# A list scheduler that merges threads by estimated times: new prices for returns to dense products, copies that count as readers, and three reorderings inside the threads

## The chip, the core and the metric

The kernel runs on one core of one Trainium2 chip. TensorE (PE) multiplies and transposes; its weight loads are shown on a line of their own (PEld). VectorE (DVE), ScalarE (ACT) and GpSimd (POOL) do the element-wise work, and most transfers between device memory and on-chip memory are issued by SyncE (SP). The metric is the time of one execution on the device in microseconds (us). The time before is the median of three runs.

## What is computed

One step of a two-layer decoder for a prompt of 2048 positions (16 tiles of 128) and 64 sample positions (8 sequences of 8), model width 1024. Both groups share all weights.

```python
# layer 0 (even): gated DeltaNet, 4 heads, beside sliding-window attention, 8 query heads / 2 kv heads
qkv_a, gate_a, a_in, b_in, q_b, k_b, v_b, gate_b = jnp.split(x @ w_in, EVEN_SPLITS, axis=-1)
qkv_a, new_conv = causal_conv(qkv_a, conv_buf, conv_w)
...
o_a, new_s = gated_delta_rule(q_a, k_a, v_a, log_decay, beta, s0)      # chunkwise, a triangular inverse per chunk
o_a = rms_norm(o_a, norm_g).reshape(n, l, A_VW) * jax.nn.silu(gate_a)
...
y = jnp.concatenate([o_a, o_b], axis=-1) @ w_out
# layer 1 (odd): HGRN2, 8 heads, 128 x 128 state each
dec = masked_exp(causal, G_c[:, :, :, None, :] - G_c[:, :, None, :, :])
a = jnp.einsum('nhid,nhijd,nhjd->nhij', q_c, dec, k_c)
o = jnp.einsum('nhid,nhde->nhie', q_c * jnp.exp(G_c), s) + jnp.einsum('nhij,nhje->nhie', a, v_c)
...
# after each layer
h = layer_norm(DEEPNORM_ALPHA * x + y, g, b)
return h + jax.nn.sigmoid(h @ w_ple_gate) * (p @ w_ple_proj)
```

The outputs are both activations and all new states and caches.

## The kernel before

**Threads and their merge.** The work is written as Python generators ("threads"), and each yields one instruction at a time. While the program is built, a loop in `run` (L525) chooses which thread goes next, so the order in which instructions stand in each engine's queue is the order in which this loop emits them. On the chip each engine then follows its own queue in order, and waits on semaphores where it needs another's result. The loop keeps an estimated clock for each engine, and for each buffer the estimated time of its last write and of its last reads. `op` (L348) gives each instruction a cost and a list of buffers read and written, `start` (L422) the earliest estimated start, and `emit` (L446) advances the clocks. Of all pending instructions the one with the lowest score goes next. For TensorE the score is the start with 700 ns of margin added to each input it reads (MARGIN, L57), less a price for a change between array modes.

**Three kinds of TensorE work.** Dense products have 128 x 128 weights and fp32r operands; a product is split in three, since each operand is held as a high and a low part. Full-size products that are not dense are the transposes (against the constant `ident`, in the trace bank<-cst,ar) and the fp32 products of the recurrences. Small products use 32 or 64 rows or columns of the array (`prod`, `sums`, `inverse`). `SWITCH` (L58) prices the change of array mode: 213 to whole, 100 to small. `STAY` (L59) adds 1000 ns to the score of whatever would lead from small back to whole. So a small product is taken ahead of a dense one even if it is ready somewhat later. The dense thread has the lowest priority: its score carries LATER, 30 ns.

**Threads of the even layer.** `dense_delta` makes four dense products for each of the 4 heads and each of 5 groups of tiles (2 or 4 tiles). `conv` consumes three of them and `dgate` one. `delta_unit` then runs `delta_core` (L1274): transposes of k and q, a ScalarE square of each 128 x 128 tile with the row sum as accumulator output (the squares go to one scrap buffer, `junk`), the decays, a triangular inverse in `inverse` (L1356: small products, a ScalarE copy, small products, a copy under a mask, for each of four sizes), the scan over the tiles, and `rms_out` (L1465), which squares again into a scrap buffer, scales, transposes and multiplies by the gate.

**Threads of the odd layer.** `hgrn_unit` runs once for each of 8 heads and 5 groups of tiles, so 40 times, at most three at a time (UNITS, L52). Its core is `hgrn_core` (L1716). `scale(s)` there multiplies one half of q and one half of k in place by running products B of the decays, and then makes the next, half as long B from it; the next scale starts with that B. `level(ps, c0, s)` copies small products under a mask into the diagonal blocks `Dv`. Between the scales of 32 and of 128 stand two ScalarE copies (KC and QC), three levels (4, 8, 16) and the scale of 64.

**After each layer.** `dense_post` makes the output projection, the norm, and the gate of the embedding; it is almost all dense products with transposes in `post_norm`.

**Memory.** An arena of 50 blocks of 1024 columns is handed out while the loop runs. There are eight PSUM banks, three of them (BANKS, L55) for dense products and five for the rest.

Of the kernel before, what the change touches and what calls it, by code (L numbers as in the profile page):

```python
# [54 lines left out]
BANKS = 3  # L55
LATER = 30
MARGIN = 700  # L57
SWITCH = {True: 213, False: 100}  # L58
STAY = 1000  # L59
WHOLE = (128, 128)  # L60
SMALL = (1, 2, 4, 8, 16)

# [74 lines left out]
def bc(ap, axis, n):  # L137

    ap = ap.unsqueeze(axis)
    shape = list(ap.shape)  # L140
    shape[axis] = n
    return ap.to_broadcast(shape)
# [24 lines left out]


class Op:
    __slots__ = ("eng", "fn", "cost", "rd", "wr", "tab", "nbytes", "mode", "place", "port")  # L170


class Ask:
# [35 lines left out]
class Sched:  # L209
    def __init__(self, tc):  # L210
        self.tc, self.nc = tc, tc.nc
        self.engines = {e: getattr(tc.nc, e) for e in ("tensor", "vector", "scalar", "gpsimd", "sync")}
        self.clk = dict.fromkeys(self.engines, 0.0)
        self.dma = 0.0
        self.tab = 0
        self.mode, self.place = WHOLE, None
        self.port = 0.0
        self.keys = {}
        self.threads = []
        self.pools = []  # L220
        self.seq = 0
        self.blocks, self.bi = [], {}
        self.mask, self.avail, self.owner = [], [], {}
        self.free_cols = 0
        self.parts = {}
        self.banks, self.bank_key = {}, {}
        self.dirty = True
        self.cur = None
# [119 lines left out]
    def op(self, eng, m, kw):  # L348
        o = Op()
        o.eng = eng  # L350
        o.tab = 0
        o.nbytes = 0
        f = getattr(self.engines[eng], m)
        o.fn = lambda: f(**kw)  # L354
        rd, wr = [], []
        src = None
        for k, v in kw.items():
            if hasattr(v, "ap") and hasattr(v, "offset"):
                if k in ("out", "accum_out", "ap"):
                    wr.append(self.key(v))  # L360
                    if k != "accum_out":
                        out = v
                else:
                    rd.append(self.key(v))
                    if src is None:
                        src = v
        o.rd, o.wr = rd, wr
        sh = out.shape
        n = 1
        for d in sh[1:]:  # L370
            n *= d
        ps_in = any(hasattr(v, "ap") and hasattr(v, "offset") and v.name in self.bank_key for k, v in kw.items() if k not in ("out", "accum_out"))
        if eng == "tensor":
            lhs = kw["in_"] if m == "transpose" else kw["lhsT"]
            o.mode = tuple(32 if x <= 32 else 64 if x <= 64 else 128 for x in (lhs.shape[0], lhs.shape[1]))
            o.place = (lhs.offset // lhs.ap[0][0], out.offset // out.ap[0][0])
            load = o.mode[1] * 0.84 + 3
            if m == "transpose":
                o.cost = max(load, n * 0.835 + 2)
            elif kw["rhs"].dtype == F32R:  # L380
                o.cost = max(load, n * 0.4258 + 8)
            else:
                o.cost = max(2 * load, n * 1.74)
        elif eng == "scalar":
            o.cost = n * 0.8333 + (51 if ps_in else 93)
            for k in ("bias", "scale"):
                if hasattr(kw.get(k), "ap"):
                    o.cost += 93
            if "accum_out" in kw:
                o.cost += 93  # L390
            o.tab = TABLE.get(kw["func"], 0)
        elif eng == "vector":
            if m in ("tensor_copy", "memset"):
                o.cost = n * (1.04 if ps_in else 0.52) + 68
            elif m == "tensor_scalar":
                o.cost = n * (1.04 if ps_in else 0.52) + 130
            elif m == "scalar_tensor_tensor":
                o.cost = n * 1.04 + 130
            elif m == "reciprocal":
                o.cost = n * 6.25 + 70  # L400
            elif m == "bn_stats":
                o.cost = 602
            else:
                o.cost = n * 1.04 + 69
        elif eng == "gpsimd":
            if m == "tensor_tensor":
                o.cost = (165 * n + 100) if kw["op"] == ALU.pow else 2.1 * n + 148
            elif m == "tensor_scalar":
                o.cost = 0.83 * n + 245
            elif m == "tensor_copy":  # L410
                o.cost = 3.4 * n + 100
            else:
                o.cost = 0.6 * n + 100

        two = sum(hasattr(kw.get(k), "ap") and kw[k].name not in self.bank_key for k in ("in_", "in0", "in1")) - (m == "transpose")
        o.port = eng == "gpsimd" and m in ("tensor_tensor", "tensor_copy") or eng == "vector" and (two == 2 or two == 1 and m in ("tensor_copy", "tensor_scalar") and out.name not in self.bank_key)
        if m == "dma_start":
            o.cost = 475.0 if eng == "sync" else 1320.0
            o.nbytes = 4 * n * sh[0]
        return o  # L420
# [25 lines left out]
    def emit(self, o, t):  # L446
        o.fn()
        c = o.cost
        if o.eng == "tensor":
            if o.mode == self.mode != WHOLE and o.place != self.place:  # L450
                c = 20 if o.mode[0] == 32 else c / 2 if o.place[1] <= self.place[1] else 14
            self.mode, self.place = o.mode, o.place
        if o.tab and not (self.tab & o.tab):
            c += 1283
        if o.tab:
# [69 lines left out]
    def run(self):  # L525
        while self.threads:
# [6 lines left out]
            for t in self.threads:  # L533
                o = t.pend
                if not isinstance(o, Op):
                    continue

                s = self.start(o, MARGIN if o.eng == "tensor" else 0, True)
                if o.eng == "tensor" and self.mode != o.mode:
                    s -= SWITCH[o.mode == WHOLE] - STAY * (o.mode == WHOLE)  # L540
                sc = s + (1283 if o.tab and not (self.tab & o.tab) else 0) + (t.prio >= 1e6) * LATER
                if best is None or sc < best[0]:
                    best = (sc, s, t)
# [9 lines left out]
def al(n, r=False):  # L553

    return Ask("mem", (n, r))
# [22 lines left out]
class Step(Sched):  # L578
# [695 lines left out]
    def delta_core(self, np_, n, cs, q, G4, maskD, small, out, own):  # L1274
# [5 lines left out]
        WT = n * 128  # L1280
        sm = yield al(128)
        ss, Gp, Gj, kds, lqk = sm[:np_, 0 : 2 * n], sm[:np_, 8 : 8 + n], sm[:np_, 16 : 16 + n], sm[:np_, 24 : 24 + n], sm[:np_, 32 : 32 + n]
        junk = yield al(128)
        psk = yield bank()
        for c in range(n):
            yield self.P.transpose(out=psk[:np_, c * 128 : (c + 1) * 128], in_=kT[:, c * cs : (c + 1) * cs], identity=self.ident)
        for c in range(n):
            yield self.A.activation(out=junk[:np_], in_=psk[:np_, c * 128 : (c + 1) * 128], func=AF.Square, accum_out=ss[:, c : c + 1])
        psq = yield bank()
        for c in range(n):  # L1290
            yield self.P.transpose(out=psq[:np_, c * 128 : (c + 1) * 128], in_=qT[:, c * cs : (c + 1) * cs], identity=self.ident)
        for c in range(n):
            yield self.A.activation(out=junk[:np_], in_=psq[:np_, c * 128 : (c + 1) * 128], func=AF.Square, accum_out=ss[:, n + c : n + c + 1])
        self.freebank(psq)
        self.free(junk)
        yield self.A.activation(out=ss, in_=ss, func=AF.Ln, bias=self.eps[:np_])
        lk, lq = ss[:, :n], ss[:, n:]
        yield self.V.scalar_tensor_tensor(out=Gp, in0=lk, scalar=-0.5, in1=G, op0=ALU.mult, op1=ALU.add)
# [15 lines left out]
        yield self.A.activation(out=lqk, in_=lqk, func=AF.Exp)  # L1314
        yield self.V.scalar_tensor_tensor(out=Gj, in0=lk, scalar=0.5, in1=GmB, op0=ALU.mult, op1=ALU.add)

        kdb = yield al(WT)
        kd = cut(kdb[:np_], 128)
        yield self.V.tensor_tensor(out=kd, in0=cut(psk[:np_, :WT], 128), in1=bc(kds, 2, 128), op=ALU.mult)
        self.freebank(psk)  # L1320
# [144 lines left out]
    def rms_out(self, np_, n, cs, po, lqk, g, sg, dst):  # L1465


        sm = yield al(256)
        f, junk = sm[:np_, 128 : 128 + n], sm[:np_, 0:128]
        for c in range(n):  # L1470
            yield self.A.activation(out=junk, in_=po[:np_, c * 128 : (c + 1) * 128], func=AF.Square, accum_out=f[:, c : c + 1])
        if lqk is not None:
            yield self.V.scalar_tensor_tensor(out=f, in0=lqk, scalar=EPS * 128 * 128, in1=f, op0=ALU.mult, op1=ALU.add)
        else:

            yield self.V.tensor_scalar(out=f, in0=f, scalar1=EPS * 128 * 4 * 128, scalar2=None, op0=ALU.add)
        yield self.G.tensor_tensor(out=f, in0=f, in1=self.mhalf[:np_, :n], op=ALU.pow)
        on = yield al(n * 128)
        yield self.V.tensor_tensor(out=cut(on[:np_], 128), in0=cut(po[:np_, : n * 128], 128), in1=bc(f, 2, 128), op=ALU.mult)
        for c in range(n):  # L1480
            yield self.P.transpose(out=po[:, c * cs : (c + 1) * cs], in_=on[:np_, c * 128 : (c + 1) * 128], identity=self.ident[:np_, :np_])
# [234 lines left out]
    def hgrn_core(self, np_, n, cs, q, k, f, deep, out, own):  # L1716
# [14 lines left out]
        def scale(s):  # L1731
# [3 lines left out]
            qv = QF.rearrange("p (b r i) -> p b r i", r=2, i=hs)  # L1735
            kv = k.rearrange("p (b r i) -> p b r i", r=2, i=hs)
            bv = B.rearrange("p (b r) -> p b r", r=2)
            yield self.V.tensor_tensor(out=qv[:, :, 1, :], in0=qv[:, :, 1, :], in1=bc(bv[:, :, 0], 2, hs), op=ALU.mult)
            yield self.V.tensor_tensor(out=kv[:, :, 0, :], in0=kv[:, :, 0, :], in1=bc(bv[:, :, 1], 2, hs), op=ALU.mult)
            if Bs is None:  # L1740
                Bs = yield al(W)
            B = Bs[:, bo : bo + nbk]
            bo += nbk
            yield self.V.tensor_tensor(out=B, in0=bv[:, :, 0], in1=bv[:, :, 1], op=ALU.mult)

        def prod(ps, c0, kk, qq):

# [60 lines left out]
        if deep:  # L1808
# [16 lines left out]
            KC, QC = (cut(KB[:, i * W // 2 : (i + 1) * W // 2], 32) for i in range(2))  # L1825
            yield self.A.activation(out=KC, in_=k.rearrange("p (b r i) -> p b r i", r=2, i=32)[:, :, 0, :], func=AF.Copy)
            yield self.A.activation(out=QC, in_=right(QF, 32), func=AF.Copy)
            for i, s in enumerate((4, 8, 16)):
                yield from level(ps, i * n * 16, s)
            self.freebank(ps)  # L1830
            yield from scale(64)
            ps = yield bank()
            for c in range(n):
                for b in range(2):
# [359 lines left out]
```

## Time and profile before

| | |
|---|---|
| median of three runs | 3127.14 us (3126.95 to 3135.73) |
| profiled execution | 3119.46 us; span from first to last instruction 3117.7 us |
| mean granted TensorE clock | 0.983 |
| instructions | 63598 |
| PE busy / PEld busy | 3002.6 us / 2498.8 us |
| DVE busy / ACT busy / POOL busy | 1964.8 us / 1228.3 us / 198.7 us |

The even layer's mixers take roughly the first 1200 us, its projection the time to about 1600 us, the odd layer's mixers the time to about 2700 us, and its projection the rest. In the profile all instructions stand under one line, L354, since one helper records each of them; they are told apart by engine, operation and shape. "128*32 128x16" of a TensorE row is the part of the array that is used, then the moving operand. A duration of a matmul there is its passage through the pipeline, not its share of the engine: consecutive starts are much closer together.

### The profile page before, as it was taken

The page shows a single profiled execution, that of the slowest core. Times are in us where ns is not written, and L with a number is a line of the kernel's source. Part 1 is how long each engine was busy: PE and PEld are TensorE (multiplying, and loading weights), DVE is VectorE, ACT ScalarE, POOL GpSimd, SP SyncE. Part 2 cuts the span into 40 slices and gives each one's busy share as a digit, 9 for nine tenths or more (in the row PEclk, how much of TensorE's full clock was granted, in tenths as well). Part 3 has the DMA queues.
Part 4 walks back from the last instruction along what each step waited for, and adds up shares of the span by engine and source line. Part 5 has one row for each costly group of instructions (what it writes and reads, how often), then busy time and mean ns, then how long its engine had stood idle before and what let it go on. Part 6 is the DMA issues. An engine that isn't in the chain of part 4 may idle for free. (4 is left out here: it accounts for less than half of the span.)

```text
span 3117.7 us, 63598 instructions
## 1 busy us (share of the span) xinstructions
PE 3002.6 (96%) x25592; PEld 2498.8 (80%) x25592; DVE 1964.8 (63%) x5693; ACT 1228.3 (39%) x3314; POOL 198.7 (6%) x265
## 2 busy tenths in 40 slices
PE   8999999999999999999999999998999999999999
PEld 7887778877787787878888888887888888787787
DVE  5567776786767675333367786868577677733333
ACT  4555555564556462101144343434444444411011
POOL 0000000000000001111100000000000000111110
PEclk9999999999999999999999999999999999999999
DMA  4221132231214154333332121222221122732331
GB/s 119 71 77 47 47 92 63 71 80 44 68 54 114 48 171 138 87 79 88 88 112 64 49 63 49 76 64 87 70 59 56 44 70 61 213 87 75 83 86 49
DMA packets 320838, 246.45 MB, mean 79 GB/s; under 512 B 33800, under 2 KB 285840, under 8 KB 320528
## 3 DMA queue, kind: packets, MB, share of 16 engines
q1 hardware_dynamic: 253408, 207.80, 22.0%
q0 software_dynamic: 67136, 34.61, 6.2%
q8 instruction: 200, 3.28, 0.4%
q14 instruction: 94, 0.77, 0.1%
HBM read 182.98 MB, written 60.45 MB: 78 GB/s over the span
## 5 line engine op out<-in xcount | busy, mean ns | idle before, releaser
L354 PE MATMUL bank<-ar,ar 128*128 128x512 f32 (+10 forms) x20432 | 2813.2, 302 | 67.2 <-ACT ar L354 39.8
L354 PEld LDWEIGHTS bank<-ar,ar 128*128 128x128 f32 (+4 forms) x20432 | 2244.8, 162 | 474.2 <-ACT ar L354 65.1
L354 ACT ACTIVATE ar<-bank 128x128 f32<-128x128 f32 (+13 forms) x1471 | 525.9, 368 | 1081.5 <-PE bank L354 998.6
L354 DVE TENSOR_TENSOR ar<-ar,ar 128x256 f32<-128x256 f32 (+8 forms) x1500 | 732.6, 517 | 247.9 <-ACT ar L354 210.3
L354 ACT ACTIVATE ar<-ar 128x512 f32<-128x512 f32 (+15 forms) x1067 | 527.8, 522 | 750.0 <-DVE ar L354 384.6
L354 DVE SCALAR_TENSOR_TENSOR ar<-ar,bank 128x512 f32<-128x512 f32 (+3 forms) x256 | 164.1, 641 | 386.6 <-ACT ar L354 254.2
L354 PE MATMUL bank<-cst,ar 128*128 128x128 f32 (+3 forms) x1439 | 239.7, 279 | 27.5 <-DVE ar L354 16.4
L354 PEld LDWEIGHTS bank<-cst,ar 128*128 128x128 f32 (+3 forms) x1439 | 173.5, 141 | 73.8 <-DVE ar L354 16.9
L354 POOL TENSOR_TENSOR ar<-ar,mhalf 128x2 f32<-128x2 f32 (+3 forms) x104 | 109.2, 1050 | 1496.8 <-DVE ar L354 1130.1
L354 DVE TENSOR_TENSOR ar<-bank,ar 128x128 fp32r<-128x128 f32 (+7 forms) x326 | 147.2, 455 | 75.7 <-ACT ar L354 43.7
L354 DVE TENSOR_TENSOR ar<-ar 128x4 f32<-128x4 f32 (+10 forms) x592 | 139.9, 250 | 19.9 <-ACT ar L354 13.3
L354 DVE SCALAR_TENSOR_TENSOR ar<-bank,ar,ar 128x509 f32<-128x509 f32 (+8 forms) x216 | 122.7, 573 | 25.8 <-ACT ar L354 24.4
L354 DVE SCALAR_TENSOR_TENSOR ar<-ar,ar,bank 128x128 f32<-128x128 f32 x192 | 65.8, 343 | 115.2 <-PE bank L354 114.6
L354 PEld LDWEIGHTS bank<-ar 32*32 32x32 f32 (+3 forms) x2640 | 88.8, 121 | 38.9 <-ACT ar L354 13.6
L354 PE MATMUL bank<-ar 32*32 32x32 f32 (+5 forms) x2640 | 113.7, 209 | 4.5 <-ACT ar L354 2.3
L354 DVE COPY_PREDICATED ar<-cst,bank 128x64 f32<-128x64 uint32 (+3 forms) x356 | 85.9, 242 | 34.9 <-PE bank L354 24.4
L354 DVE SCALAR_TENSOR_TENSOR ar<-ar,ar,ar 128x1024 f32<-128x1024 f32 (+1 forms) x68 | 87.0, 1280 | 13.8 <-POOL ar L354 13.8
L354 POOL MEMSET ar<- 128x256 f32 (+4 forms) x85 | 29.1, 348 | 961.1 <-PE bank L354 550.6
L354 DVE SCALAR_TENSOR_TENSOR ar<-ar,ar 128x4 f32<-128x4 f32 (+10 forms) x190 | 58.4, 312 | 31.7 <-ACT ar L354 30.5
L354 POOL DMA_DIRECT2D ar<-os x64 | 57.3, 898 | 296.9 <-PE bank L354 197.0
L354 ACT ACTIVATION_READ_ACCUMULATOR ar<-bank 128x1 f32 (+1 forms) x340 | 66.2, 195 | 0.0
L354 ACT ACT_TABLE_LOAD x49 | 62.9, 1283 | 5.5 <-DVE ar L354 4.0
(55 smaller groups left out, 799.9 us busy)
## 6 DMA issues: line engine op xcount, KB each, us to landing
ar<-os POOLq DMA_DIRECT2D x64, 512.0 KB, 5.0
ar<-in_w_in_odd SPq DMA_DIRECT2D x64, 512.0 KB
ar<-in_w_in_even SPq DMA_DIRECT2D x60, 512.0 KB
os<-ar SPq DMA_DIRECT2D x36, 512.0 KB
ar<-x SPq DMA_DIRECT2D x32, 512.0 KB
os<-ar SPq DMA_DIRECT2D x56, 256.0 KB
ar<-in_x_prompt SPq DMA_DIRECT2D x16, 512.0 KB
ar<-in_w_ple_gate SPq DMA_DIRECT2D x16, 512.0 KB
```

What stands on the lines that cost most here:

```text
L354: o.fn = lambda: f(**kw)
```

## The change

It alters the merge's prices and three places in the threads. No instruction is added or taken away.

1. Prices. `SWITCH` becomes 105 to whole and 120 to small. A new mark `dense` on each TensorE instruction tells fp32r products of whole size from all others. A dense product that follows one that was not dense is charged `BACK`, 90 ns, on the estimated clock. `STAY` becomes a pair: 900 ns on the score of what leads from small to whole, and 300 ns on the score of a dense product that follows a whole-size one that is not dense.
2. A copy under a mask (`copy_predicated`) is now listed as a reader of its own output, so that the estimate lets it start 127 ns after the last write of that buffer on the same engine.
3. In `delta_core` and `rms_out` the squares no longer share one 128-column scrap: each goes to a slice of its own in a buffer that is needed later anyway (`kdb`, `on`), which is allocated earlier for it.
4. In `scale` the running product B is made between the multiplication of q and that of k.
5. In `hgrn_core` the three masked levels and the three instructions of the scale of 64 are interleaved, a scale first.

```diff
-SWITCH = {True: 213, False: 100}
-STAY = 1000
+SWITCH = {True: 105, False: 120}
+BACK = 90
+STAY = (900, 300)
...
+        if m == "copy_predicated":
+            rd.append(self.key(kw["out"]))
...
+            o.dense = o.mode == WHOLE and m != "transpose" and kw["rhs"].dtype == F32R
...
-            self.mode, self.place = o.mode, o.place
+            if o.dense and not self.was_dense:
+                c += BACK
+            self.mode, self.place, self.was_dense = o.mode, o.place, o.dense
...
-                if o.eng == "tensor" and self.mode != o.mode:
-                    s -= SWITCH[o.mode == WHOLE] - STAY * (o.mode == WHOLE)
+                if o.eng == "tensor":
+                    if self.mode != o.mode:
+                        s -= SWITCH[o.mode == WHOLE] - STAY[0] * (o.mode == WHOLE)
+                    elif o.dense and not self.was_dense:
+                        s += STAY[1]
...
-        junk = yield al(128)
+        kdb = yield al(WT)
...
-            yield self.A.activation(out=junk[:np_], in_=psk[:np_, c * 128 : (c + 1) * 128], func=AF.Square, accum_out=ss[:, c : c + 1])
+            yield self.A.activation(out=kdb[:np_, c * 128 : (c + 1) * 128], in_=psk[:np_, c * 128 : (c + 1) * 128], func=AF.Square, accum_out=ss[:, c : c + 1])
...
-        sm = yield al(256)
-        f, junk = sm[:np_, 128 : 128 + n], sm[:np_, 0:128]
+        sm = yield al(128)
+        f = sm[:np_, :n]
+        on = yield al(n * 128)
         for c in range(n):
-            yield self.A.activation(out=junk, in_=po[:np_, c * 128 : (c + 1) * 128], func=AF.Square, accum_out=f[:, c : c + 1])
+            yield self.A.activation(out=on[:np_, c * 128 : (c + 1) * 128], in_=po[:np_, c * 128 : (c + 1) * 128], func=AF.Square, accum_out=f[:, c : c + 1])
...
-            yield self.V.tensor_tensor(out=qv[:, :, 1, :], in0=qv[:, :, 1, :], in1=bc(bv[:, :, 0], 2, hs), op=ALU.mult)
-            yield self.V.tensor_tensor(out=kv[:, :, 0, :], in0=kv[:, :, 0, :], in1=bc(bv[:, :, 1], 2, hs), op=ALU.mult)
...
+            yield self.V.tensor_tensor(out=qv[:, :, 1, :], in0=qv[:, :, 1, :], in1=bc(bv[:, :, 0], 2, hs), op=ALU.mult)
             yield self.V.tensor_tensor(out=B, in0=bv[:, :, 0], in1=bv[:, :, 1], op=ALU.mult)
+            yield self.V.tensor_tensor(out=kv[:, :, 0, :], in0=kv[:, :, 0, :], in1=bc(bv[:, :, 1], 2, hs), op=ALU.mult)
...
-            for i, s in enumerate((4, 8, 16)):
-                yield from level(ps, i * n * 16, s)
+            masked = iter([level(ps, i * n * 16, s) for i, s in enumerate((4, 8, 16))])
+            for o in scale(64):
+                yield o
+                yield from next(masked)
             self.freebank(ps)
-            yield from scale(64)
```

More of the change, by code (lines that the diff above doesn't have):

```diff
@@ L169 @@
 class Op:
-    __slots__ = ("eng", "fn", "cost", "rd", "wr", "tab", "nbytes", "mode", "place", "port")
+    __slots__ = ("eng", "fn", "cost", "rd", "wr", "tab", "nbytes", "mode", "place", "port", "dense")
 class Ask:
@@ L215, in __init__ @@
         self.tab = 0
-        self.mode, self.place = WHOLE, None
+        self.mode, self.place, self.was_dense = WHOLE, None, True
         self.port = 0.0
@@ L1292, in delta_core @@
         for c in range(n):
-            yield self.A.activation(out=junk[:np_], in_=psq[:np_, c * 128 : (c + 1) * 128], func=AF.Square, accum_out=ss[:, n + c : n + c + 1])
+            yield self.A.activation(out=kdb[:np_, c * 128 : (c + 1) * 128], in_=psq[:np_, c * 128 : (c + 1) * 128], func=AF.Square, accum_out=ss[:, n + c : n + c + 1])
         self.freebank(psq)
-        self.free(junk)
         yield self.A.activation(out=ss, in_=ss, func=AF.Ln, bias=self.eps[:np_])
@@ L1315, in delta_core @@
         yield self.V.scalar_tensor_tensor(out=Gj, in0=lk, scalar=0.5, in1=GmB, op0=ALU.mult, op1=ALU.add)
-        kdb = yield al(WT)
         kd = cut(kdb[:np_], 128)
@@ L1477, in rms_out @@
         yield self.G.tensor_tensor(out=f, in0=f, in1=self.mhalf[:np_, :n], op=ALU.pow)
-        on = yield al(n * 128)
         yield self.V.tensor_tensor(out=cut(on[:np_], 128), in0=cut(po[:np_, : n * 128], 128), in1=bc(f, 2, 128), op=ALU.mult)
```

## The prediction

> **What bounds the kernel now.** I read the page's busy times first, then the busy time by stage, then the list of what TensorE waited for.
>
> ```profile
> PE 3002.6 (96%) x25592; PEld 2498.8 (80%) x25592; DVE 1964.8 (63%) x5693; ACT 1228.3 (39%) x3314; POOL 198.7 (6%) x265
> ```
>
> ```profile
> 28.00:1200.00 1172.00, 1111.93 (x10962) 913.08 (x10961) 817.28 (x2690) 635.25 (x1795) 38.34 (x65) 0.97 0.28 77
> 1600.00:2706.00 1106.00, 1071.74 (x10894) 920.07 (x10894) 815.43 (x2478) 480.32 (x1313) 69.71 (x112) 0.99 0.24 71
> 2706.00:3112.00 406.00, 405.71 (x1843) 329.42 (x1842) 154.13 (x236) 44.04 (x81) 46.79 (x44) 1.00 0.34 82
> 2167.00:2196.00 29.00, 18.64 (x165) 11.64 (x163) 22.20 (x88) 10.91 (x36) 2.02 (x5) 0.65 0.53 155
> ```
>
> ```profile
> PE bank L354 <- DVE ar L354: 54.3, 92, 3.1
> PE bank L354 <- ACT ar L354: 48.0, 46, 7.3
> PE bank L354 <- DMA ar<-x: 4.5, 2, 4.3
> ```
>
> The columns of the second fence are the stretch, its length, the busy time of PE, PEld, DVE, ACT and POOL, then the granted clock and the DMA. TensorE is the bound: idle 60.1 us of the even mixers' 1172.0, 34.3 us of the odd mixers' 1106.0, and 0.3 us of the last projection's 406.0. Nothing of the change can help that last stage. What an element-wise edit can win lies in the third fence: 102.3 us in 138 waits for DVE and ACT, 0.74 us each on average. Some of this costs twice. In the 29 us between the two halves of the odd layer TensorE is idle for 10.4 us and the clock granted is 0.65, so about 10 us more is lost to the clock. The merge's order decides everything else: how often TensorE changes between kinds of work, and what that costs.
>
> **The change, part by part.** The number of instructions stays the same on every engine, and so do the DMAs.
>
> *Returns from transposes and fp32 products to dense ones.* The new price is 90 ns. The timeline of TensorE shows what a return costs:
>
> ```profile
> 606.76 0.38 PE L354 MATMUL bank<-cst,ar 128*128 128x128 f32 x2
> 606.89 0.36 PE L354 MATMUL bank<-ar,ar 128*128 128x256 f32 x1
> 607.09 0.82 PE L354 MATMUL bank<-cst,ar 128*128 128x128 f32 x6
> 607.67 0.36 PE L354 MATMUL bank<-ar,ar 128*128 128x256 f32 x1
> 607.87 0.60 PE L354 MATMUL bank<-cst,ar 128*128 128x128 f32 x4
> 608.22 2.26 PE L354 MATMUL bank<-ar,ar 128*128 128x256 f32 x15
> 610.41 0.44 PE L354 MATMUL bank<-cst,ar 128*128 128x128 f32 x2
> ```
>
> The first column is the start; the next start tells how long the engine was taken. Two transposes take 0.13 us (606.76 to 606.89), six 0.58, four 0.35: each further one 0.11, and the last of a burst only about 0.02. The single dense product behind a burst takes 0.20 us, where the 15 from 608.22 take 0.146 each with the first one's excess and a stray slow one among them. So the first dense product does start a slow interval, some 0.08 us, but the last transpose before it is shorter by as much. From 606.76 to 607.87 there are eight transposes and two products: 1.11 us measured, against 8 x 0.11 + 2 x 0.114 (half of a 512-wide product, below) to 0.146 = 1.11 to 1.17 without any return. I price a return at 0, with 0.01 as the upper bound. A dense product that waits for more transposes therefore wins nothing, and the 90 ns on the estimated clock tells the merge that TensorE is slower than it is.
>
> *Trips to small products.* These do cost:
>
> ```profile
> 2372.60 0.60 PE L354 MATMUL bank<-cst,ar 128*128 128x128 f32 x4
> 2372.95 8.00 PE L354 MATMUL bank<-ar,ar 128*128 128x512 f32 x34
> 2380.88 0.86 PE L354 MATMUL bank<-ar,cst 128*32 128x128 f32 x24
> 2381.67 4.84 PE L354 MATMUL bank<-ar,ar 128*128 128x512 f32 x20
> 2386.45 0.45 PE L354 MATMUL bank<-ar 128*32 128x16 f32 x32
> ...
> 2999.72 10.59 PE L354 MATMUL bank<-ar,ar 128*128 128x512 f32 x46
> ```
>
> In the last row 46 products run undisturbed: 10.59 us, with 0.4 for the passage of the last one through the pipeline (a lone 256-wide one above has 0.36), so 0.227 each. The two dense runs above both end in a change to small. The first begins behind four transposes. Its 34 products would take 7.72 of their 7.93, so 0.21 is left, of which 0.08 is the refunded interval above and 0.13 the change to small. The 20 behind the small ones take 4.78, 0.24 over 4.54: the return from small costs 0.11. With what the small run itself loses at its end, estimated at another 0.1, a trip is worth 0.24 to 0.35 us. STAY falls from 1000 to 900, so the merge lets TensorE wait in small mode 100 ns less: a few more trips at 0.3 against a few fewer waits of 0.2 to 0.3. I take 0, with 30 trips either way (9 us) as the bounds.
>
> *Scrap buffers.* A square into `junk` waits for the square before it:
>
> ```profile
> 47.04 0.18 ACT L354 ACTIVATION_READ_ACCUMULATOR ar<-ar,ar 128x1 f32 x1
> 47.13 0.49 ACT L354 ACTIVATE ar<-ar,ar 128x256 f32<-128x256 f32 x1
> ...
> 2248.91 0.19 ACT L354 ACTIVATION_READ_ACCUMULATOR ar<-bank 128x1 f32 x1
> 2249.13 0.28 ACT L354 ACTIVATE ar<-bank 128x128 f32<-128x128 f32 x1
> ```
>
> ```profile
> L354 ACT ACTIVATION_READ_ACCUMULATOR ar<-bank 128x1 f32 x320 | 62.4, 195 | 0.0
> ```
>
> The attention's exponentials, each in its own place, start 0.09 us after the accumulator read; the squares 0.22. Of 320 squares of full tiles 220 follow another one of their group (60 groups in the delta units, 40 in the odd units), so 220 x 0.13 = 29 us of ScalarE goes. ScalarE is at 39%, hidden by TensorE nearly everywhere. What counts is 0.13 to 0.39 us off the chain that leads from the scan to the transposes in `rms_out`, and from k's transposes to the decays. The new uses of `kdb` and `on` put a wait before the first square, for whoever had the larger buffer last; the planner counts that as a buffer request, and behind it stand only the unit's own squares. I price it at 0, at most the 0.13 saved.
>
> *Masked copies and scalings.*
>
> ```profile
> 2226.32 1.09 DVE L354 TENSOR_TENSOR ar<-ar 128x256 f32<-128x256 f32 x3
> ...
> 2229.98 0.97 DVE L354 COPY_PREDICATED ar<-cst,bank 128x64 f32<-128x64 uint32 x3
> ...
> 2234.03 0.18 DVE L354 TENSOR_TENSOR ar<-ar 128x32 f32<-128x32 f32 x1
> 2234.69 0.76 DVE L354 TENSOR_TENSOR ar<-ar,ar 128x256 f32<-128x256 f32 x2 [0.48 <-PE bank L354]
> 2235.36 0.17 DVE L354 TENSOR_TENSOR ar<-ar 128x16 f32<-128x16 f32 x1
> 2235.45 0.75 DVE L354 COPY_PREDICATED ar<-cst,bank 128x64 f32<-128x64 uint32 x3
> 2236.32 0.76 DVE L354 TENSOR_TENSOR ar<-ar,ar 128x256 f32<-128x256 f32 x2
> ```
>
> ```profile
> 2229.98 0.30 DVE L354 COPY_PREDICATED ar<-cst,bank 128x64 f32<-128x64 uint32 x1
> 2235.03 0.42 DVE L354 TENSOR_TENSOR ar<-ar,ar 128x256 f32<-128x256 f32 x1
> ```
>
> Three multiplications of 0.42 us take 1.09, so one starts 0.08 before the other's end. Three copies of 0.30 take 0.97: each starts 0.03 after the other's end. The wait for one's own predecessor is 0.12 us. Interleaving removes two such waits a unit, and making B earlier removes one for each scale whose next scale follows at once, up to five; the rows at 2234.03 and 2234.69 show that there the wait for TensorE ends last, so little of it counts. For 40 units that is 9.6 to 34 us of DVE, of 1964.8 busy. A price stands against it: the scale of 64 now heads the three copies, and its first multiplication has to wait for the ScalarE copy of q (QC), with the first masked copy queued behind it. What follows next, the products of 64, needs the scale, so its chain gets no longer; the PSUM bank comes free up to 0.8 us later (two multiplications, the row at 2236.32), one of five.
>
> The Trainium skill, page "VectorE: DVE Perf Modes", section "The DRAIN you can't avoid", says that a semaphore after each of eight copies costs nothing over one after the last. By that rule this part would be worth nothing; the trace disagrees, with 0.03 after against 0.08 before the end.
>
> *What reaches the end.* The two last parts shorten chains that TensorE waits for. If half of the 138 waits lie behind such a step and each shrinks by 0.13 us, that is 9 us; the bounds are 0 and 27 us (all of them by 0.2). In slow-clock stretches such as 2167 to 2196 a us less of waiting brings up to a us of clock: I take 3 us. Returns 0, trips 0. **Sum: -12 us, so 3107.5 us for the profiled execution of 3119.46, and 3115 us against the median 3127.14**, which lies 7.7 us above the profiled one. A difference of 0.3%, 9.4 us, is about what a measurement of this kernel can tell from no change.
>
> **Rivals.**
>
> *The return does cost 90 ns.* For it: the 0.20 us interval of a lone dense product. Against it: the refund in the transpose before, and the sum of 1.11 us.
>
> ```profile
> L354 PE MATMUL bank<-cst,ar 128*128 128x128 f32 x1340 | 222.1, 281 | 17.5 <-DVE ar L354 9.0 <-DMA ar<-x 4.5 <-ACT ar L354 3.7
> ```
>
> In bursts of two to six, 1340 transposes make 220 to 670 returns. If 140 are avoided, that is 12.6 us beside the 12: 3102 us. Page "TensorEngine Tiling (Array Packing)" of the Trainium skill, section "Key Properties", has a drain only where the tiling mode changes, which a transpose of full size does not do; the rows agree.
>
> *It is all hidden.* For it: TensorE is 96% busy, and the merge already fills most waits with dense products, so that shorter chains only give idle time on engines that have 37% and 61% of it. Then the time stays near 3127 us, with a few us either way from another order.
>
> *The hold spends the margin (slower).* After a transpose or fp32 product a dense one is now scored 300 ns later. So another thread's product is taken ahead of it once its input is estimated ready 400 ns before, not 700. The estimate knows neither the granted clock nor what a queue in front costs, and it now takes TensorE to be up to 0.08 us later at each return than it is. Where the input comes late, TensorE stands in order, with dense products ready behind it. A wait now costs 0.74 us on average. With 16 more of these the -12 is gone; with 45 more, one in 5 to 15 of the returns, the time is 3127 - 12 + 33 = 3148 us. That waits in the trace number only 138 in all speaks against it: the margin of 700 was rarely spent.
>
> **How the numbers follow.** Forecast, faster by 0.3 to 1%, centre 3115: 0.34. Returns really dear, 3102 or below: 0.11. All hidden, 3118 to 3136: 0.30. Slower by the margin, centre 3148: 0.25. So faster 0.45, same 0.30, slower 0.25. The sum's bounds are 3127 - 27 - 3 - 9 = 3088 at the fast end, which takes in most of the second case, and at the slow end half of the last case is wanted: 3150. The range is 3088 to 3150, and the forecast's own 3096 to 3118.
>
> **What would show it.** Returns: bursts of transposes get longer and single dense products between them rarer, while eight transposes and two products still take 1.1 us. Scrap: a square starts 0.09 us after the accumulator read. Masked copies: no run of three, and DVE's busy rows between them overlap. The sum is right if the waits of TensorE for DVE and ACT fall from 102.3 to about 93 us. It is wrong if these grow, if trips to small products change by more than 30, or if the clock in the stretch between the halves moves by itself.

## The result

The changed kernel takes 3095.61 us (median of four runs, 3091.01 to 3105.41) against 3127.05 before (3125.88 to 3135.73). The ratio is 0.9898, 95% interval 0.9868 to 0.9927: 31 us faster, where 12 were forecast. The profiled execution was the longest of the four, 3105.41 us with a span of 3103.6, so its rows show only about half of the gain.

The page's busy times of the changed kernel, and below them what TensorE waited for (us in total, times, longest):

```profile
PE 2998.2 (97%) x25592; PEld 2502.7 (81%) x25592; DVE 1958.4 (63%) x5693; ACT 1212.5 (39%) x3316; POOL 195.9 (6%) x265
```

```profile
PE bank L355 <- DVE ar L355: 44.6, 63, 4.2
PE bank L355 <- ACT ar L355: 40.6, 40, 7.5
PE bank L355 <- DMA ar<-x: 9.7, 2, 5.7
```

The waits for DVE and ScalarE fell from 102.3 us in 138 to 85.2 us in 103; those for the DMA of x rose from 4.5 to 9.7 us. ScalarE's busy time fell by 15.8 us, less than the 29 us of waits between squares: some 0.03 us in front of each held square was idle already, 7 us in all, and two more table loads (51 for 49, 1.28 us each) take 2.6. The remaining difference, some 4 us, is not accounted for. The squares, in the timeline of ScalarE, first one start of the kernel before and then the changed kernel:

```profile
2249.53 0.28 ACT L354 ACTIVATE ar<-bank 128x128 f32<-128x128 f32 x1
```

```profile
2240.52 0.28 ACT L355 ACTIVATE ar<-bank 128x128 f32<-128x128 f32 x1 [3.50 <-PE bank L355]
2240.69 0.20 ACT L355 ACTIVATION_READ_ACCUMULATOR ar<-bank 128x1 f32 x1
2240.79 0.27 ACT L355 ACTIVATE ar<-bank 128x128 f32<-128x128 f32 x1
2240.95 0.20 ACT L355 ACTIVATION_READ_ACCUMULATOR ar<-bank 128x1 f32 x1
2241.04 0.28 ACT L355 ACTIVATE ar<-bank 128x128 f32<-128x128 f32 x1
```

A square now starts 0.09 to 0.10 us after the accumulator read, as the exponentials did, and the next one 0.26 us after it instead of 0.40 (2249.13, in the prediction's rows, to 2249.53). The masked copies, in the timeline of DVE:

```profile
2227.80 0.43 DVE L355 TENSOR_TENSOR ar<-ar,ar 128x256 f32<-128x256 f32 x1 [0.87 <-ACT ar L355]
2228.15 0.22 DVE L355 COPY_PREDICATED ar<-cst,bank 128x64 f32<-128x64 uint32 x1
2228.28 0.16 DVE L355 TENSOR_TENSOR ar<-ar 128x8 f32<-128x8 f32 x1
2228.40 0.22 DVE L355 COPY_PREDICATED ar<-cst,bank 128x64 f32<-128x64 uint32 x1
2228.54 0.42 DVE L355 TENSOR_TENSOR ar<-ar,ar 128x256 f32<-128x256 f32 x1
2228.88 0.22 DVE L355 COPY_PREDICATED ar<-cst,bank 128x64 f32<-128x64 uint32 x1
```

Scale and copies alternate, and each starts before the one in front has ended. Of the masked copies of this shape, 42 still follow another one directly, where it was 96: `hgrn_core` has an earlier group of three that the change leaves as it was. The price foreseen for the new order is there too: the scale waits 0.87 us for the ScalarE copy, with the first masked copy queued behind it.

On TensorE the stretches of dense products, counted in the trace (a stretch begins where a dense product, here a whole-size one of 256 columns or more, follows another kind), fell from 1019 to 852, and those of a single product from 135 to 36. The trips to small products stayed, 430 before and 432 after. So the planner did what its prices ask for: the hold gathers transposes. Whether the gain comes from that was the question for the runs.

### The profile page after: what moved, and what is told of

Its sections match the earlier page's. It is cut to its first block, busy times and chain, and to the rows that moved or that the text cites. A ratio compares the mean times of both kernels' runs of the same rounds, so it can differ in the third digit from the quotient of the medians.

```text
span 3103.6 us, 63559 instructions
## 1 busy us (share of the span) xinstructions
PE 2998.2 (97%) x25592; PEld 2502.7 (81%) x25592; DVE 1958.4 (63%) x5693; ACT 1212.5 (39%) x3316; POOL 195.9 (6%) x265
## 5 line engine op out<-in xcount | busy, mean ns | idle before, releaser
L355 PEld LDWEIGHTS bank<-ar,ar 128*128 128x128 f32 (+5 forms) x20622 | 2254.5, 162 | 475.5 <-issue 74.6
L355 ACT ACTIVATE ar<-bank 128x128 f32<-128x128 f32 (+14 forms) x1471 | 522.3, 369 | 1125.0 <-PE bank L355 1051.5
L355 DVE TENSOR_TENSOR ar<-ar,ar 128x256 f32<-128x256 f32 (+11 forms) x1511 | 749.6, 515 | 273.8 <-ACT ar L355 230.8
L355 ACT ACTIVATE ar<-ar 128x1024 fp32r<-128x1024 f32 (+15 forms) x1071 | 532.9, 524 | 699.9 <-DVE ar L355 325.4
L355 PE MATMUL bank<-cst,ar 128*128 128x128 f32 (+4 forms) x1439 | 239.0, 282 | 19.0 <-DMA ar<-x 9.7
L355 PEld LDWEIGHTS bank<-cst,ar 128*128 128x128 f32 (+4 forms) x1439 | 172.4, 142 | 62.7 <-DVE ar L355 10.6
L355 DVE TENSOR_TENSOR ar<-bank,ar 128x128 fp32r<-128x128 f32 (+8 forms) x326 | 147.4, 455 | 64.8 <-ACT ar L355 39.8
L355 DVE TENSOR_TENSOR ar<-ar 128x256 f32<-128x256 f32 (+11 forms) x581 | 138.7, 251 | 19.0 <-ACT ar L355 16.6
L355 PE MATMUL bank<-ar 32*32 32x32 f32 (+6 forms) x2450 | 106.4, 208 | 5.9 <-DVE ar L355 2.6
L355 PEld LDWEIGHTS bank<-ar 128*32 128x32 f32 (+3 forms) x2450 | 84.1, 122 | 31.1 <-issue 10.9
L355 DVE SCALAR_TENSOR_TENSOR ar<-ar,ar,ar 128x1024 f32<-128x1024 f32 (+1 forms) x68 | 87.0, 1280 | 13.6 <-POOL ar L355 13.4
```

## The experiments

Three theories were set against each other. **A**, the prediction's: a return to dense products is free, and the gain is in chains of ScalarE and DVE that TensorE waits for. **B**: fewer returns are the gain. **C**: any change of a price gives another order, and orders differ by some 0.3% without a mechanism. After the first eight runs A was narrowed to the scrap buffers (A2), and B to a gain of the hold that does not come from a return's price (B2).

### The prices alone

```diff
-SWITCH = {True: 213, False: 100}
-STAY = 1000
+SWITCH = {True: 105, False: 120}
+BACK = 90
+STAY = (900, 300)
```

with the code that uses them, as in the change.

> The kernel before with the new prices alone (SWITCH, BACK, STAY), threads as before. Theory A, the prediction's (a return costs nothing, the gain is in shorter chains of DVE and ScalarE): 3125 us, within 0.3% of the kernel before, dense stretches fewer by some 150 but TensorE's busy time the same within 3 us. Theory B (fewer returns and joined trips are what is won): 3100 us, and TensorE's time outside its waits shorter by 15 us or more. Theory C (any new order moves the time by about 0.5% either way, without a mechanism): anywhere from 3110 to 3145 us.

Measured: 3136.18 us, ratio 1.0019 (1.0004 to 1.0035). What TensorE waited for:

```profile
PE bank L355 <- DVE ar L355: 71.9, 108, 4.2
PE bank L355 <- ACT ar L355: 38.6, 44, 7.7
```

There are 886 dense stretches instead of 1019, and still no gain: B, which expected 3100 us, falls for the prices by themselves. The waits for DVE rose from 54.3 us to 71.9. That is the prediction's slower rival, the hold that spends the margin, in a milder form: 8 us more waits in all.

### The three thread edits alone

```diff
+            yield self.A.activation(out=kdb[:np_, c * 128 : (c + 1) * 128], in_=psk[:np_, c * 128 : (c + 1) * 128], func=AF.Square, accum_out=ss[:, c : c + 1])
...
+            yield self.V.tensor_tensor(out=B, in0=bv[:, :, 0], in1=bv[:, :, 1], op=ALU.mult)
...
+            masked = iter([level(ps, i * n * 16, s) for i, s in enumerate((4, 8, 16))])
```

> The kernel before with the three thread edits alone (own places for the squares, B between the scalings, masked copies among the scalings), prices as before. Theory A: about 3105 us, TensorE's waits for DVE and ScalarE down from 102 to about 85 us. Theory B: 3122 to 3127 us. Theory C: anywhere from 3110 to 3145 us.

Measured: 3107.01 us, ratio 0.9923 (0.9902 to 0.9943), as A expected. B, with 3122 to 3127 us, falls here too. Waits for DVE and ScalarE: 52.3 + 42.3 = 94.6 us, where A expected about 85.

### Masked copies as readers, alone

```diff
+        if m == "copy_predicated":
+            rd.append(self.key(kw["out"]))
```

> The kernel before with masked copies listed as readers of their output, and nothing else. All the instructions and their dependences are those of before, only the estimate differs. Theory A: 3120 to 3127 us (the estimate is 0.12 us truer per copy, little more). Theory B: 3127 us. Theory C: anywhere from 3110 to 3145 us.

Measured: 3116.45 us, ratio 0.9953 (0.9936 to 0.9970). By itself that reads like a gain of 13 us, but see the control that ran beside it.

### A control: near-ties decided otherwise

```diff
-LATER = 30
+LATER = 40
```

> A control: the kernel before with LATER at 40 instead of 30 ns, so that near-ties of the merge fall otherwise and nothing else. Theories A and B: within 0.3% of the kernel before, 3118 to 3136 us. Theory C: off by 0.3 to 0.6%, to either side.

Measured: 3119.81 us, ratio 0.9964 (0.9948 to 0.9980). Ten ns on a tie-break, which change nothing but the order, are worth some 10 us. The interval is narrow, so this is no scatter of the measurement but another order. From here on an effect of some 10 us between two orders counts as nothing shown, the one of the readers included.

### The changed kernel with the old prices

```diff
-SWITCH = {True: 105, False: 120}
-BACK = 90
-STAY = (900, 300)
+SWITCH = {True: 213, False: 100}
+STAY = 1000
```

> The changed kernel with the old prices back (SWITCH 213 and 100, STAY 1000, no charge and no hold for a return); masked copies as readers and the three thread edits stay. Theory A (the gain is in the shorter chains and the truer copies, the new prices give nothing): 3085 to 3098 us, not slower than the changed kernel at 3095.6. Theory B (the new prices belong to the gain): 3105 to 3115 us. Theory C (each order is a draw with a spread of about 0.3%): 3095 to 3115 us, no rule.

Measured: 3125.43 us, ratio 0.9990 (0.9977 to 1.0003). A expected 3085 to 3098 and is wrong here, and the time lies above the ranges of B and C as well: readers and thread edits together, with the old prices, are no faster than before, though the thread edits alone were at 3107. The readers, which change only the estimate, go with 13 us less on the kernel before and with 18 us more on the thread edits: orders differ by more than the control had shown. The new prices, which lost 7 us alone, go with 30 us less on top of the rest. Either they gain by another way than the price of a return, or this order is a poor one.

### Squares in places of their own, alone

```diff
-        sm = yield al(256)
-        f, junk = sm[:np_, 128 : 128 + n], sm[:np_, 0:128]
+        sm = yield al(128)
+        f = sm[:np_, :n]
+        on = yield al(n * 128)
```

and the same with `kdb` in `delta_core`.

> The kernel before with places of their own for the squares, and nothing else. Theory A: about 3115 us, half of the 22 us that the thread edits gave together; the squares start 0.09 instead of 0.22 us after the accumulator read, 29 us of ScalarE's time goes. Theory C: as the control, 3110 to 3130 us, with the ScalarE effect there all the same.

Measured: 3106.79 us, ratio 0.9928 (0.9912 to 0.9944). A expected 3115. This edit alone gives the whole of what the three gave together, and ScalarE's busy time is 1202.6 us, 25.7 less than before.

```profile
PE bank L354 <- DVE ar L354: 46.9, 85, 3.6
PE bank L354 <- ACT ar L354: 41.8, 41, 7.6
```

The waits fall by 13.6 us, from 102.3 to 88.7.

### Masked copies and scalings, alone

```diff
+            yield self.V.tensor_tensor(out=B, in0=bv[:, :, 0], in1=bv[:, :, 1], op=ALU.mult)
...
+            for o in scale(64):
+                yield o
+                yield from next(masked)
```

> The kernel before with B between the scalings and the masked copies among the scalings of 64, and nothing else. Theory A: about 3115 us, and the gain is in the odd layer's mixers (the stage from 1600 to 2706 us), none in the even layer, which the edit does not touch. Theory C: 3110 to 3130 us, and stages that the edit does not touch move as much as the one that it does.

Measured: 3125.46 us, ratio 0.9992 (0.9979 to 1.0005): no change that can be measured. A expected 3115. Waits 57.0 + 46.2 = 103.2 us, as before. Little DVE time was saved that could have been hidden:

```profile
PE 3003.4 (96%) x25592; PEld 2499.7 (80%) x25592; DVE 1963.7 (63%) x5693; ACT 1228.7 (39%) x3314; POOL 196.5 (6%) x265
```

DVE was busy for 1964.8 us before. Only 41 masked copies stand directly behind another, but 910 DVE instructions start 0.02 to 0.06 us after the end of the one in front, and in the kernel before it was 910 too. So as many wait as before, whatever the new order takes away; where the others arise is not shown.

### Set patterns on TensorE

A tail after all other work of the changed kernel runs fixed sequences of transposes (T), dense products (D) and small products (S), with nothing to wait for, and 24 products of 384 columns between patterns.

```diff
+PROBE = [
+    (1, (("T", 48, 0), ("D", 48, 512))),
+    (12, (("T", 4, 0), ("D", 4, 512))),
+    (48, (("T", 1, 0), ("D", 1, 512))),
...
+    (12, (("S", 16, 0), ("T", 4, 0), ("D", 4, 512))),
...
+    (12, (("T", 4, 0), ("D", 2, 512), ("S", 16, 0), ("D", 2, 512))),
+]
```

> The changed kernel with a tail that runs set patterns on TensorE after all other work: 48 transposes and 48 dense products of 512 columns in one burst each, in fours, and one by one; the same with 256 columns; 192 small products and 48 dense ones in one burst and in twelve; and transposes, small products and dense ones in three orders. If a return is free: the three first patterns take the same within 0.5 us, 16.2 us each (48 x 0.11 + 48 x 0.227). If a return costs 90 ns: fours take 1.0 us more than one burst, and one by one 4.2 us more. Trips to small: twelve take 11 x 0.24 to 0.35, 2.6 to 3.9 us, more than one.

The timeline of TensorE in that tail:

```profile
3108.04 5.40 PE L367 MATMUL bank<-cst,ar 128*128 128x128 f32 x48
3113.20 15.34 PE L367 MATMUL bank<-ar 128*128 128x512 f32 x72
3128.38 0.60 PE L367 MATMUL bank<-cst,ar 128*128 128x128 f32 x4
3128.73 1.17 PE L367 MATMUL bank<-ar 128*128 128x512 f32 x4
3129.74 0.60 PE L367 MATMUL bank<-cst,ar 128*128 128x128 f32 x4
...
3143.27 0.60 PE L367 MATMUL bank<-cst,ar 128*128 128x128 f32 x4
3143.63 5.33 PE L367 MATMUL bank<-ar 128*128 128x512 f32 x28
3148.80 0.27 PE L367 MATMUL bank<-cst,ar 128*128 128x128 f32 x1
3148.82 0.48 PE L367 MATMUL bank<-ar 128*128 128x512 f32 x1
3149.14 0.27 PE L367 MATMUL bank<-cst,ar 128*128 128x128 f32 x1
...
3164.92 4.64 PE L367 MATMUL bank<-ar 128*128 128x512 f32 x25
...
3244.98 0.66 PE L367 MATMUL bank<-cst,ar 128*128 128x128 f32 x4
3245.39 1.55 PE L367 MATMUL bank<-ar 128*128 128x512 f32 x36
3246.87 0.66 PE L367 MATMUL bank<-cst,ar 128*128 128x128 f32 x4
...
3271.46 0.60 PE L367 MATMUL bank<-cst,ar 128*128 128x128 f32 x4
3271.99 1.58 PE L367 MATMUL bank<-ar 32*32 32x32 f32 x36
3273.41 0.60 PE L367 MATMUL bank<-cst,ar 128*128 128x128 f32 x4
...
3299.02 0.60 PE L367 MATMUL bank<-cst,ar 128*128 128x128 f32 x4
3299.38 1.74 PE L367 MATMUL bank<-ar 128*128 128x512 f32 x36
3300.96 0.60 PE L367 MATMUL bank<-cst,ar 128*128 128x128 f32 x4
```

Forty-eight transposes take 5.16 us; with 0.03 for the last one that is 0.109 for each of the others. Four and four take (3143.27 - 3128.38) / 11 = 1.354 us, against 4 x 0.109 + 4 x 0.227 = 1.344. One and one take (3164.92 - 3148.82) / 47 = 0.343, against 0.336. **A return costs 0.007 to 0.010 us, not 0.09.** The 167 dense stretches fewer of the changed kernel are worth 1 to 2 us. The last three groups are the same work in three orders: S, T, D takes 1.90 us a round, T, S, D takes 1.95 (3271.46 to 3273.41), and T, two D, S, two D takes 1.94. So joining kinds saves nothing by itself, and the orders differ by 0.05. Sixteen small products with their trip cost 0.55 to 0.60 us, the 1.90 to 1.95 less the 1.35 of four and four.

What a trip costs can be read from two other stretches, a burst of small products and eleven rounds of 16 small and 4 dense ones:

```profile
3199.86:3202.02 2.16, 2.16 (x259) 2.16 (x260) 0.00 (x0) 0.00 (x0) 0.00 (x0) 1.00 0.00 0
3222.30:3238.90 16.60, 16.60 (x397) 11.17 (x396) 0.00 (x0) 0.00 (x0) 0.00 (x0) 1.00 0.01 3
```

A small product is two entries of the trace, so the first row holds 8 x 16 of them: 0.27 us for 16. A round takes 16.60 / 11 = 1.51, and the trip 1.51 - 0.27 - 4 x 0.227 = 0.33 us. That lies in the prediction's 0.24 to 0.35. (Later in its burst of small products TensorE stands still for 2.18 us, with nothing in the profile that it waits for; the first row ends before that.)

### The control on the other side

```diff
-LATER = 30
+LATER = 40
```

in the changed kernel.

> The control on the other side: the changed kernel with LATER at 40 instead of 30 ns, nothing else. Theory A2 (the gain belongs to the scrap buffers, which alone gave 22 us, and is steady): 3090 to 3108 us. Theory C (the order is a draw with a spread of about 10 us; 3095.6 is a good one): 3105 to 3120 us.

Measured: 3103.78 us, ratio 0.9920 (0.9902 to 0.9938). The changed kernel stays faster than before under another order, 8 us above its own median. But the kernel to hold it against is the control, which has the same LATER: 3119.81 to 3103.78 is 16 us, half of the 31 with LATER at 30.

### The squares again, beside the control

The scrap edit with LATER at 40.

> The kernel before with places of their own for the squares and LATER at 40, to be held against the control without them (LATER 40 alone, 3119.8 us). Theory A2: 3098 to 3108 us, 12 to 22 us below that control. Theory C: anywhere from 3100 to 3130 us, the effect not the same as with LATER at 30.

Measured: 3100.26 us, ratio 0.9902 (0.9889 to 0.9916), 19.5 us below the control without the edit. With LATER at 30 it was 22. Under two orders the edit gives nearly the same, as A2 expected. It is also 3.5 us faster than the whole change with LATER at 40, so under that order prices, readers and masked copies add nothing to the scrap.

How much of the 20 us is the shorter chain is not shown, since the edit changes the merge's order as well: from 239 us on TensorE gets its products in another order than before. The traces separate the layers. Up to the odd layer's first small product (128*32 128x16), with time at halved clock counted half, the edit saves 6.0 us with LATER at 30 and 5.3 with 40. From there to that layer's last one it saves 14.8 and 5.7; but there the readers alone, which leave the first part's order as it was, save 15.6. So 5 to 6 us up to the odd layer are the same under both orders; what is saved in the odd layer is no more than orders differ by. An edit of the scrap with every queue's order kept would settle it and was not run.

### The changed kernel without the hold

```diff
-STAY = (900, 300)
+STAY = (900, 0)
```

> The changed kernel without the hold of 300 ns (the second STAY 0), the charge of 90 ns and the other prices kept. Theory B2 (the hold gains by another way than the price of a return, since without the new prices the time was 3125): 3115 to 3125 us, dense stretches back at about 1000. Theory A2: 3095 to 3105 us. Theory C: anywhere from 3095 to 3125 us.

Measured: 3120.63 us, ratio 0.9974 (0.9963 to 0.9984), 25 us above the changed kernel, with 996 dense stretches. That is what B2 expected, and C's range (3095 to 3125) takes it in too. The waits for DVE and ScalarE:

```profile
PE bank L355 <- DVE ar L355: 52.9, 73, 3.3
PE bank L355 <- ACT ar L355: 41.9, 46, 7.6
```

94.8 us, 9.6 above the changed kernel's.

### The changed kernel without the charge

```diff
-BACK = 90
+BACK = 0
```

> The changed kernel without the charge of 90 ns on the estimated clock (BACK 0), hold and other prices kept. By the tail with set patterns a return costs 0.006 to 0.011 us, so this estimate is the truer one. Theories A2 and B2: 3090 to 3100 us, not slower than the changed kernel. If the charge itself helps, by keeping the estimate of TensorE back where the clock or queues slow it: 3105 us or more. Theory C: anywhere from 3095 to 3125 us.

Measured: 3085.06 us (3080.29 to 3087.32), ratio 0.9854 (0.9841 to 0.9866). It beats both kernels. Hold and new prices stay; only the charge is gone that the set patterns show to be wrong.

```profile
PE bank L355 <- DVE ar L355: 44.1, 72, 3.1
PE bank L355 <- ACT ar L355: 39.3, 36, 7.7
```

Against the changed kernel it is 10 us faster, no more than the control moved, so that the truer estimate is the cause is not shown; that the charge isn't needed is. The kernel has 874 dense stretches.

### Together

| scrap | hold | medians, us | waits for DVE and ScalarE, us |
|---|---|---|---|
| shared | no | 3127 (before), 3116 (readers), 3120 (control), 3125 (masked) | 96.9 to 103.2 |
| shared | yes | 3136 (prices) | 110.5 |
| own | no | 3107 (scrap), 3107 (threads), 3100 (scrap, LATER 40), 3125 (old prices), 3121 (no hold) | 88.7 to 101.7 |
| own | yes | 3096 (changed), 3104 (LATER 40), 3085 (no charge) | 83.4 to 92.4 |

The rows' means are 3122, 3136, 3112 and 3095 us; within a row the kernels lie up to 25 us apart. So own scrap is worth 10 us without the hold on average (and 20 to 22 in both pairs that differ in nothing else), and the hold about 17 where the scrap is its own. The rows differ in more than their names say: the kernels that hold have the new `SWITCH` too, and readers and `BACK` vary. With shared scrap the one kernel that holds is slower, and at LATER 40 the one with its own scrap is no faster (3104) than the scrap without it (3100). Time and waits go together down the table, but the fall of the waits is only about half of the fall of the time.

## Why the prediction was right

**Direction and range.** Faster was forecast as the likeliest, and 3095.6 lies in the range of 3088 to 3150, just outside the forecast's own 3096 to 3118. The gain is 2.6 times the sum. The scrap alone, one of its terms, is faster under both orders; that the whole gain is so large is in part luck of the order, since with LATER at 40 the same change is worth 16 us, close to the 12 of the sum.

**Returns at 0: right.** The set patterns give 0.007 to 0.010 us, at the upper bound of 0.01 that the prediction took from eight transposes and two products. The refund that it read (a short last transpose before a long first interval) is what they show. The rival "the return does cost 90 ns" ends at 3102, near the measured time, but for a wrong reason: the prices alone reduce the dense stretches by 133 and give no gain.

**A hold "therefore wins nothing": not settled.** Its price was right; whether the conclusion was is open. With LATER at 30 the kernel without the hold is 25 us slower than the changed one, more than the 18 us that the readers alone move the thread edits by. With LATER at 40 the whole change with its hold is no faster than the scrap alone. If the hold gains, it is not by a return's price: it lets waiting transposes go ahead of dense products, so that the chains on DVE and ScalarE that start from them start sooner. The waits agree (94.8 us without the hold, 85.2 with it) for 10 of the 25 us. That mechanism is argued, not shown, and a kernel without the hold at LATER 40 was not run.

**Scrap: mechanism right, size too small.** The stall between squares went as read, from 0.22 to 0.09 us after the read. Its share of the 9 us was put low because ScalarE is at 39%; the edit alone gave 22 us and, under another order, 19.5. That is inside the bound of 27, which the prediction had for the two last parts together. In waits the fall is 13.6 and 10.1 us (102.3 to 88.7, and 100.3 to 90.2 with LATER at 40), nearer to the sum. The term takes half of the 138 waits at 0.13 us, where a group of four squares shortens its chain by 0.4; that this is why it came out small is argued. The rest of the 20 us is not separated from the other order that the edit brings.

**Masked copies and scalings: no gain shown.** Foreseen as part of the 9 us; alone 3.7 us with an interval that includes none. The separation is in the trace, but of the 9.6 to 34 us of DVE that the prediction counted the busy time shows 1.1, in the changed kernel 6.4. That step failed: with the edit alone DVE waits for its predecessor as often as before. Where the new order stands, what ends the unit's next step can be ScalarE or TensorE (0.87 us at 2227.80). The rule that the prediction quotes from the Trainium skill, page "VectorE: DVE Perf Modes", section "The DRAIN you can't avoid", gave the right total here by a wrong way: the wait between dependent copies is in the rows (0.03 us after the end against 0.08 before it).

**Trips at 0: right as far as counted.** 430 trips to small before, 432 after, and 0.33 us for one where 0.24 to 0.35 was read.

**The slower rival: there, but not alone.** The prices alone raise the waits by 8 us and the time by 7 to 9. Where the squares are set apart as well that loss does not show.

**The clock: not the one read.** The profiled execution after has a lower granted clock (0.980 against 0.983), and in the stretch between the halves of the odd layer it was halved for 27 us (2161 to 2188) instead of 20 (2173 to 2194). So the 3 us put down for it are not confirmed.

**Not foreseen: the scatter of orders.** A tie-break moves the time by 10 us, and the readers, which change only the estimate, by 13 us one way and 18 the other. The prediction's "few us either way from another order" was too small, and part of the 31 us can't be told from that.

## What to carry to other kernels

Where instructions that write only to throw away share one scrap, they wait for each other; give each its own place in a buffer that is needed later anyway, even on an engine that is mostly idle, if another engine waits for its chain. Price a transition by the time of a whole round, not by the one interval that looks long: the neighbour may be shorter by as much. And where a planner orders the work, run controls that change only a tie-break, on both sides of the change, before believing an effect under one per cent.

## What the runs showed of the hardware

The same program's time follows the granted clock from run to run. The four timed executions of the changed kernel had spans of 3103.6, 3094.1, 3093.6 and 3089.2 us at mean clocks of 0.980, 0.983, 0.983 and 0.984; span times clock is 3041.5, 3041.5, 3041.0 and 3039.8. The clock has three digits, so a product is good to 2 us. So 14 us between executions of one kernel, nearly half of what the change is worth, go with the clock. For the kernel before, the profiled 3117.7 us at 0.983 make 3064.7: at full clock the change is worth some 23 us. The kernel before had a mean clock of 0.980 over 28 executions beside the first four experiments, the changed one 0.9825 over its four; 0.0025 of 3100 us is the 8 us that are left.

By the same product other differences come out smaller. The hold shrinks from 25 us to 16 (3057 to 3041), the scrap from 22 and 19.5 to 17 and 11 (3066 to 3049, and 3059 to 3048 with LATER at 40), and the whole change at LATER 40 from 16 to 2 (3059 to 3057). Whether a kernel's clock differs by its order or by chance is not shown: in the same set of runs it was 0.980 for the kernel before and without the hold, 0.984 to 0.986 for the other three.
